# Conversions of the second layer's weights one step behind their raw loads, and the samples' norm with tokens on partitions

## The chip, the cores and the metric

The kernel runs on one core of one Trainium2 chip. The metric is the device time of one execution in microseconds (us). Before the change the median of three runs is 2826.94 us (2825.27 to 2832.05). All engines of the core work at once, each through its own list of instructions in a fixed order: TensorE (PE in the profile; its weight loads are PEld), VectorE (DVE), ScalarE (ACT), GpSimd (POOL) and SyncE (SP), which here only issues transfers.

## The reference

One inference step of a two-layer decoder for two groups of tokens that share the weights: a prompt of 2048 tokens and 8 samples of 4 tokens each (32 rows). The model width is 1024.

- Layer 0 is gated linear attention with 4 heads (keys of 128, values of 512): `o, state = gla_recurrence(q, k, v, log_a, state0)`, then `o = rmsnorm(o, out_norm_g)` per head, then `(o * silu(gate)) @ w_out`. The samples start from given states, the prompt from zero.
- Keys and values for layer 1 are projected once from the residual after layer 0 (`w_k`, `w_v`).
- Layer 1 is sliding-window attention (128 previous positions and the token itself) with 32 query heads of 64 in 4 groups: `q, gate = split(rmsnorm(h) @ b_w_in)`, attention with sinks, `(o * silu(gate)) @ b_w_out`.

The two places that the change touches are the weights of layer 1 (`w_k`, `w_v`, `b_w_in`), which have to be brought into the form that the matmuls read, and the per-head `rmsnorm` of the samples' readout `o` in layer 0: the mean of 512 squares for each of the 32 tokens, to the power -1/2, times `o`.

## The kernel before, in words

All large matmuls work on numbers split into two 16-bit halves, a high and a low one (`split`, L185 to L193): ScalarE writes the high half with one activation (L189 or L192), VectorE writes the rest, the difference, as the low half (L190 or L193). A product is three passes of 16-bit matmuls (`PASSES`).

A `Unit` (L195 on) is a piece of 1024 weight columns in two halves of 512. `Unit.convert` (L207) takes one half: it loads the raw 32-bit numbers into a tile `wraw` of 128x512 (three buffers) with one or two transfers from SyncE's queue, and splits them, scaled by the gain of the norm, into the tile that it is given. For layer 0's weights this tile is a `W` tile that stays on the chip (`load`, L230). Layer 1's weights don't fit beside layer 0's, so `prepare` (L235) converts them in advance: it takes a tile `pst` (two buffers), calls `convert`, and writes `pst` to a tensor `pre` in the chip's memory with a transfer from GpSimd's queue (L243). Much later `fetch` loads the finished pieces in one transfer each. There are 72 such halves: 8 of `w_k` and `w_v` (two transfers each) and 64 of `b_w_in`.

Work in layer 0 runs in 16 blocks: for each head h (4) the four quarters j of the prompt (512 tokens). A block projects v and the gate for four chunks of 128 tokens and q and k of the block after it, takes seven masked `lev` products (`level_steps`), and runs the state recurrence (`chunk_steps`). The last quarter of each head (j = 3) also projects the samples (`SampleA.proj_steps`) and loads the next head's `W` tiles; the samples' own recurrence (`SampleA.steps`: `diag`, `level`, `mid`, `stack`, eight times `seq`, `fin`) is spread over the first quarter of the next head (for the last head over the first chunks of the output projection). It uses `pst` tiles too: `stack`, each `seq` and `fin` take one.

After the last block come 16 chunks of layer 0's output projection (`a_out`), then layer 1.

Where the order of the work comes from: the program is written as lists of steps that `weave` lays into each other, and a planner (`TileContext(nc, schedule_with_timeline_sim=True)`) then makes each engine's list from it, by priorities and by its own durations for every instruction and transfer. Steps in `behind(steps, n)` have their priority lowered by n. What is ready early by the planner's reckoning may be moved ahead of what stands before it in the program; `tc.keep_in_program_order` forbids this for one instruction: it adds an order-only edge from the instruction of the same engine that precedes it in the program text.

The preparation of layer 1's weights is a list `prep` of small steps (L869): 8 steps for the rotary tables, the 72 halves of `prepare`, each lowered by 200, and 64 steps that form combinations of `b_w_out`. `some(n)` takes the next n steps; each chunk of a block takes `PR[j]` of them, that is 1, 4, 2 and 0 for j = 0 to 3 (none in the first two blocks and in the last two), and chunks 1 to 3 of the output projection six each. So by the program text 3, 12 and 6 steps fall into the first three quarters of a head.

`fin` of the samples (L784 to L801) for one head: the readout `ot` (128 value rows on the partitions, 4 pieces, 32 tokens along the free axis) is squared on ScalarE; four 32-bit matmuls with a 128x128 matrix of ones as the moved-against operand (`mm(pq, onef, sq[:, x])`) give the sum of squares of each token in all 128 partitions; VectorE scales it (L796), GpSimd raises 128x32 numbers to the power -1/2 (L797), and VectorE multiplies the gate and the readout (L799) and the result by the power (L800).

## Time and profile before

| | |
|---|---|
| median of the runs | 2826.94 us (2825.27 to 2832.05, three runs) |
| the profiled execution | 2821.32 us, of which 2819.5 us lie between its first and last instruction |
| mean granted TensorE clock | 0.988 |
| 0 to 340 us | head 0 with its loads and norms: PE busy 297.15 us |
| 340 to 1260 us | heads 1 to 3 and the first chunks of the output projection: PE busy 886.63 of 920 us |
| 1260 to 1500 us | rest of the output projection: PE busy 239.76 of 240 us |
| 1500 to 2819.5 us | layer 1 |

How to read it. The span is the time from the first to the last instruction of one profiled execution. A row of the windows view gives, for one stretch of the span, how long each engine was busy in it and the clock that TensorE was granted. A row of a timeline has the start, the duration, the engine, the line, and the tile written and the tiles read; a bracket at its end gives the idle time of that engine just before, and what ended it. "DMA pre<-pst" is a transfer from a `pst` tile, "L218 wraw<-in_b_w_in_dram" the raw load of a half.

### The profile page before, as it was taken

The page shows a single profiled execution, that of the slowest core. Times are in us where ns is not written, and L with a number is a line of the kernel's source. Part 1 is how long each engine was busy: PE and PEld are TensorE (multiplying, and loading weights), DVE is VectorE, ACT ScalarE, POOL GpSimd, SP SyncE. Part 2 cuts the span into 40 slices and gives each one's busy share as a digit, 9 for nine tenths or more (in the row PEclk, how much of TensorE's full clock was granted, in tenths as well). Part 3 has the DMA queues.
Part 4 walks back from the last instruction along what each step waited for, and adds up shares of the span by engine and source line. Part 5 has one row for each costly group of instructions (what it writes and reads, how often), then busy time and mean ns, then how long its engine had stood idle before and what let it go on. Part 6 is the DMA issues. An engine that isn't in the chain of part 4 may idle for free.

```text
span 2819.5 us, 51844 instructions
## 1 busy us (share of the span) xinstructions
PE 2712.2 (96%) x19258; PEld 1388.1 (49%) x19258; DVE 1699.8 (60%) x3470; ACT 1394.2 (49%) x3245; POOL 1150.2 (41%) x1600
## 2 busy tenths in 40 slices
PE   6899999999999999999999999999999999989999
PEld 3444544544454445445444555555555555544444
DVE  5555666566556654346413666677777767777653
ACT  6554656455546554434312555566666666651110
POOL 2442244223323421236304686566557657530000
PEclk9999999999999999999999999999999999999999
DMA  8462445135423543789856787978978889896431
GB/s 213 94 148 50 116 130 163 49 105 154 131 57 105 173 115 93 211 256 287 244 167 161 130 153 151 228 133 152 198 143 149 169 181 183 166 222 197 151 110 57
DMA packets 814470, 429.53 MB, mean 152 GB/s; under 512 B 649600, under 2 KB 723144, under 8 KB 814184
## 3 DMA queue, kind: packets, MB, share of 16 engines
q1 hardware_dynamic: 801256, 390.49, 58.9%
q0 software_dynamic: 10880, 35.66, 3.5%
q8 instruction: 150, 2.46, 0.4%
q14 instruction: 104, 0.85, 0.1%
q10 hardware_dynamic: 2080, 0.07, 0.0%
HBM read 178.75 MB, written 107.54 MB: 102 GB/s over the span
## 4 chain that ended last, share of the span: by engine, by line
PE 62%; ACT 8%; DMA 7%; issue 7%; DVE 6%; POOL 5%; SPq 1%; ACTq 0%; POOLq 0%; DVEq 0%
PE pj L102 36%; PE o L102 11%; PE tr L102 10%; PE kv L102 3%; DMA pre<-pst 2%; ACT o L1264 2%; PE lev L102 2%; DVE v L193 1%; ACT v L192 1%; DMA pst<-v 1%; POOL ogT L190 1%; DMA uT<-ogT 1%; DVE o L1259 1%; DVE lev L1259 1%; POOL rs_r L182 1%
## 5 line engine op out<-in xcount | busy, mean ns | idle before, releaser
L102 PE MATMUL pj<-W,uT 128*128 128x512 f16 x5088 | 1207.2, 382 | 7.8 <-ACT sg L482 6.0
L102 PEld LDWEIGHTS <-uT 128*128 128x128 f16 x6976 | 651.7, 98 | 714.4 <-issue 44.2
L102 PE MATMUL tr<-W,uT 128*128 128x512 f16 x1536 | 365.5, 379 | 0.0
L181 POOL TENSOR_SCALAR rs_m<-ss 128x1 f32<-128x1 f32 (+3 forms) x186 | 42.8, 230 | 548.4 <-DVE ss L1161 190.1
L102 PEld LDWEIGHTS <-X 128*128 128x128 f16 x2744 | 184.7, 98 | 140.4 <-issue 11.4
L1264 ACT ACTIVATE o<-o,mx 128x256 f32<-128x256 f32 (+1 forms) x384 | 168.7, 439 | 168.6 <-DVE mx L1259 164.7
L1259 DVE CUSTOM_DVE_ANT_0 o<-o,madd,nsink 128x256 f32<-128x256 f32 (+1 forms) x384 | 183.7, 478 | 44.6 <-PE o L102 40.4
L102 PE MATMUL pj<-uT,W 128*128 128x512 f16 (+1 forms) x912 | 186.1, 352 | 25.3 <-DMA uT<-ogT 24.4
L193 DVE SCALAR_TENSOR_TENSOR v<-o,v 128x512 f16<-128x512 f32 (+1 forms) x192 | 128.9, 671 | 104.0 <-ACT v L192 101.3
L182 POOL TENSOR_TENSOR rs_r<-rs_m,mhalf 128x1 f32<-128x1 f32 (+3 forms) x182 | 185.5, 1020 | 13.6
L515 POOL TENSOR_TENSOR KQ<-KQ,bt 128x256 f32<-128x256 f32 x112 | 97.5, 870 | 213.1 <-DVE X L190 213.1
L102 PEld LDWEIGHTS <-W 128*128 128x128 f16 x2448 | 127.7, 98 | 111.6 <-issue 19.1
L102 PEld LDWEIGHTS <-v 128*128 128x128 f16 x976 | 96.0, 99 | 120.4 <-issue 9.9
L190 POOL TENSOR_TENSOR ogT<-og,ogT 128x512 f16<-128x512 f32 x68 | 80.8, 1189 | 133.7 <-ACT ogT L189 133.7
L102 PEld LDWEIGHTS <-sg 128*128 128x128 f16 x800 | 77.8, 98 | 92.5
L189 ACT ACTIVATE X<-KQ 128x512 f16<-128x512 f32 x128 | 84.5, 660 | 74.1 <-PE lev L102 53.3
L190 DVE TENSOR_TENSOR X<-KQ,X 128x512 f16<-128x512 f32 x128 | 99.6, 778 | 28.0 <-ACT X L189 25.5
L102 PE MATMUL o<-gl,X 128*128 128x256 f16 (+1 forms) x768 | 114.4, 272 | 1.9 <-DMA gl<-KVd 1.2
L192 ACT ACTIVATE v<-o 128x512 f16<-128x512 f32 (+1 forms) x192 | 111.2, 579 | 3.5
L243 POOL DMA_DIRECT2D pre<-pst x72 | 51.1, 725 | 144.5 <-DVE pst L193 85.8
L1264 ACT ACTIVATE lev<-lev,mx 128x256 f32<-128x256 f32 (+1 forms) x128 | 56.5, 441 | 103.3 <-DVE mx L1259 101.2
L102 PE MATMUL pj<-W,v 128*128 128x512 f16 x448 | 105.6, 383 | 0.0
(437 smaller groups left out, 4848.9 us busy)
## 6 DMA issues: line engine op xcount, KB each, us to landing
pre<-pst POOLq DMA_DIRECT2D x72, 256.0 KB, 3.6
W<-pre SPq DMA_DIRECT2D x36, 512.0 KB
ogd<-ogk SPq DMA_DIRECT2D x68, 256.0 KB
wraw<-in_a_w_in_dram SPq DMA_DIRECT2D x64, 256.0 KB
wraw<-in_b_w_in_dram SPq DMA_DIRECT2D x64, 256.0 KB
oge<-og SPq DMA_DIRECT2D x64, 256.0 KB
wraw<-in_a_w_out_dram SPq DMA_DIRECT2D x32, 256.0 KB
X<-in_x_prompt_dram SPq DMA_DIRECT2D x32, 256.0 KB
```

Of the source, the lines that this page charges most:

```text
L102: return order(nc.tensor.matmul(*a, **k))
L181: pool.tensor_scalar(m[:n, :k], ss, a, b, ALU.mult, ALU.add)
L182: pool.tensor_tensor(r[:n, :k], m[:n, :k], mhalf[:n, :k], ALU.pow)
L189: act(hi, src, AF.Copy)
L190: eng.tensor_tensor(lo, src, hi, ALU.subtract)
L192: act(hi, src, AF.Copy, scale=sc)
L193: dve.scalar_tensor_tensor(lo, src, sc, hi, ALU.mult, ALU.subtract)
L243: nc.gpsimd.dma_start(self.pre[:, :, half * 512 : half * 512 + 512], t)
L515: pool.tensor_tensor(keys, keys, d[:, :, 1:2].to_broadcast([P, NB, m]), ALU.mult)
L1259: dve.tensor_tensor_reduce(pm[:, z], pm[:, z], madd.rearrange("p a b -> p (a b)")[:, (2 - nk) * P :], -0.125, nsink[:, g * GRP + h : g * G ...
L1264: act(pm[:, z], pm[:, z], AF.Exp, scale=-1.0, bias=nm_[:, h : h + 1], accum_out=bx["sum"][:, h : h + 1])
```

## The change

`Unit.convert` is cut into `raw`, which issues the raw loads, and `convert`, which splits. A step of `prepare` now issues its own raw load, then runs what the step before it left in the list `pending`, and leaves its own conversion there: the `pst` tile, the split and the write to `pre`. A `flush` step behind the last half runs what is left, so `prep` has one step more. The ScalarE activation of these conversions, and only of these, is passed through `tc.keep_in_program_order`. The conversions of layer 0's weights (`load`) keep raw load and split in one step, and are not held in program order.

In the samples' `fin` the four matmuls change their operands: the squares are now the loaded matrix and one column of ones the moving one, so that the sums of the 32 tokens stand on 32 partitions, one number each. They are copied to `ss` (VectorE), scaled and raised to the power -1/2 by `rsqrt` (L179 to L183, GpSimd, one number on each of 32 partitions), spread on a 32x32 diagonal `dg` (VectorE), and brought back to all 128 partitions by a fifth matmul `pr`, with ones; the last product reads `pr` in place of the tile `k1`.

```diff
-    def split(dst, src, sc=None, eng=dve):
+    def split(dst, src, sc=None, eng=dve, put=lambda x: x):
...
-            act(hi, src, AF.Copy, scale=sc)
+            put(act(hi, src, AF.Copy, scale=sc))
             dve.scalar_tensor_tensor(lo, src, sc, hi, ALU.mult, ALU.subtract)
+
+    pending = []
+
+    def flush():
+        while pending:
+            pending.pop(0)()
...
-        def convert(self, half, dst):
+        def raw(self, half):
...
+            return raw
+
+        def convert(self, half, raw, dst, put=lambda x: x):
...
         def load(self, half):
...
-            self.convert(half, lambda hl: self.t[:, hl, half * 512 : half * 512 + 512])
+            self.convert(half, self.raw(half), lambda hl: self.t[:, hl, half * 512 : half * 512 + 512])
...
             def one(half):
-                t = T("pst", [P, 2, 512], F16, 2)
-                self.convert(half, lambda hl: t[:, hl])
-                nc.gpsimd.dma_start(self.pre[:, :, half * 512 : half * 512 + 512], t)
+                raw = self.raw(half)
+                flush()
+
+                def rest():
+                    t = T("pst", [P, 2, 512], F16, 2)
+                    self.convert(half, raw, lambda hl: t[:, hl], tc.keep_in_program_order)
+                    nc.gpsimd.dma_start(self.pre[:, :, half * 512 : half * 512 + 512], t)
+
+                pending.append(rest)
...
-                pq = PT("tr", [P, SMP], bufs=2)
+                pq = PT("tr", [SMP, 1], bufs=2)
                 for x in range(4):
-                    mm(pq, onef, sq[:, x], start=x == 0, stop=x == 3)
+                    mm(pq, sq[:, x], onef[:, 0:1], start=x == 0, stop=x == 3)
                 k2 = SOG**-2.0
-                r = T("k1", [P, SMP], F32, 2)
-                dve.tensor_scalar(r, pq, k2 / DV, k2 * EPS * OA * OA * DK, ALU.mult, ALU.add)
-                pool.tensor_tensor(r, r, mhalf[:, 0:1].to_broadcast([P, SMP]), ALU.pow)
+                ss = T("ss", [P, 3], F32, 4)
+                dve.tensor_copy(ss[:SMP, 0:1], pq)
+                r = rsqrt(ss[:SMP, 0:1], SMP, k2 / DV, k2 * EPS * OA * OA * DK)
+                dg = T("k1", [SMP, SMP], F32, 2)
+                dve.tensor_scalar(dg, idf[:SMP, :SMP], r[:SMP, 0:1], None, ALU.mult)
+                pr = PT("tr", [P, SMP], bufs=2)
+                mm(pr, onef[:SMP], dg, start=True, stop=True)
...
-                dve.tensor_tensor(sg, sg, r.unsqueeze(1).to_broadcast([P, 4, SMP]), ALU.mult)
+                dve.tensor_tensor(sg, sg, pr.unsqueeze(1).to_broadcast([P, 4, SMP]), ALU.mult)
...
-    prep = [f for w in gw for f in w.prepare()] + [f for m in range(8) for f in form_steps(m)]
+    prep = [f for w in gw for f in w.prepare()] + behind([flush], 200) + [f for m in range(8) for f in form_steps(m)]
```

## The prediction

> **What bounds the kernel now.** I read the page first, then the windows by stage and by block, then the gaps of TensorE (PE) one by one, and for each what ScalarE (ACT) was doing.

> ```profile
> span 2819.5 us, 51844 instructions
> PE 2712.2 (96%) x19258; PEld 1388.1 (49%) x19258; DVE 1699.8 (60%) x3470; ACT 1394.2 (49%) x3245; POOL 1150.2 (41%) x1600
> ```

> PE is the bound, and the change takes no PE work away that counts, so it can only win PE's idle time and the time in which PE's clock is halved. The windows by block of heads 1 to 3 (cut where PE starts the projections of a block) say where these lie:

> ```profile
> core 0: us, PE busy (x) PEld busy (x) DVE busy (x) ACT busy (x) POOL busy (x), PEclk, DMA share, GB/s
> ...
> 415.00:485.00 70.00, 63.42 (x361) 29.13 (x360) 47.67 (x74) 45.03 (x75) 34.39 (x54) 0.98 0.59 173
> 485.00:553.00 68.00, 68.00 (x406) 32.42 (x405) 30.71 (x49) 27.72 (x47) 16.89 (x27) 1.00 0.18 43
> ...
> 688.00:757.00 69.00, 64.07 (x358) 29.21 (x357) 45.74 (x71) 39.80 (x69) 30.96 (x45) 0.95 0.60 176
> 757.00:825.00 68.00, 68.00 (x421) 32.68 (x420) 30.25 (x49) 28.08 (x48) 16.98 (x27) 1.00 0.20 42
> 825.00:888.00 63.00, 62.83 (x493) 31.87 (x490) 40.90 (x66) 38.77 (x70) 17.18 (x29) 1.00 0.41 113
> ...
> 961.00:1030.00 69.00, 61.86 (x355) 28.50 (x353) 46.43 (x67) 39.87 (x66) 25.57 (x38) 0.98 0.59 171
> ...
> 1155.00:1255.00 100.00, 92.17 (x477) 42.51 (x475) 39.07 (x79) 37.49 (x71) 16.89 (x31) 0.95 0.74 227
> ```

> The second quarter of each head (415, 688, 961) loses 6.58, 4.93 and 7.14 us, 18.65 together; the first output chunks (1155 to 1255) lose 7.83; the third quarters (485, 757) lose nothing. To the idle time comes the halved clock behind it:

> ```profile
> 444.60:448.00 3.40, 3.40 (x9) 1.22 (x8) 2.61 (x4) 0.72 (x1) 2.05 (x3) 0.50 0.93 265
> 714.20:717.60 3.40, 3.04 (x8) 1.12 (x8) 2.59 (x5) 0.70 (x1) 2.68 (x4) 0.51 0.98 223
> ...
> 1175.00:1181.90 6.90, 5.97 (x17) 2.33 (x18) 2.25 (x8) 2.54 (x7) 0.00 (x0) 0.51 0.46 125
> 1219.40:1222.80 3.40, 3.40 (x10) 1.24 (x9) 0.26 (x2) 0.88 (x4) 0.75 (x2) 0.51 0.93 311
> sum 23.90, PE 22.61 PEld 8.34 DVE 12.86 ACT 7.53 POOL 7.32; mean PE 3.77 PEld 1.39 DVE 2.14 ACT 1.25 POOL 1.22
> ```

> At half clock half of the busy time is lost: 22.61/2 = 11.3 us over these stretches, of which the two output-chunk rows hold (5.97+3.40)/2 = 4.7 and the second quarters the other 6.6. So the second quarters cost 18.65+6.6 = 25.3 us, the first output chunks 7.83+4.7 = 12.5. These 37.8 us are the most that the change can win. What PE waited for in the larger gaps:

> ```profile
> 442.47 0.38 PE L102 MATMUL kv<-v,ke 128*128 128x512 f16 x1 [2.02 <-ACT v L192]
> 712.88 0.38 PE L102 MATMUL kv<-v,ke 128*128 128x512 f16 x1 [1.40 <-ACT v L192]
> ...
> 1175.93 0.25 PE L102 MATMUL lev<-ssm 128*96 128x16 f16 x1 [3.82 <-ACT ssm L189]
> 1218.30 0.38 PE L102 MATMUL kv<-ke,skn 96*128 96x512 f16 x1 [3.91 <-DVE bt L778]
> ```

> And what ACT did meanwhile, at two of them:

> ```profile
> 441.21 0.72 ACT L192 ACTIVATE pst<-wraw,gsb 128x512 f16<-128x512 f32 x1 [0.80 <-ACT ogT L189]
> 441.84 0.58 ACT L192 ACTIVATE v<-pj 128x512 f16<-128x512 f32 x1
> ...
> 1209.80 0.69 POOL L243 DMA_DIRECT2D pre<-pst  x1 [5.57 <-DVE pst L193]
> 1210.96 0.34 SPq L218 DMA_DIRECT2D wraw<-in_b_w_in_dram  x1
> 1215.98 0.72 ACT L192 ACTIVATE pst<-wraw,gsb 128x512 f16<-128x512 f32 x1 [3.41 <-DMA pre<-pst]
> ```

> A conversion of a layer-1 half stood at the head of ACT's list, waiting for its input or its `pst` buffer, and the activation that PE needed (`v` at 441.84) stood behind it. At 1215.98 the bracket names the write from `pst`, but that was issued at 1209.80; the raw load issued at 1210.96 is the later of the two, and I take it for the real releaser: 5.0 us from issue to use.

> **The change part by part.** First where conversions run. Rows of the `wraw` tile by stretch:

> ```profile
> 417.00:485.00 68.00, 16.17 (x23) 14.04 (x23) 0.00 (x0) 0.97 0.58 171
> 485.00:553.00 68.00, 0.00 (x0) 0.00 (x0) 0.00 (x0) 1.00 0.18 43
> ...
> 676.00:744.00 68.00, 18.57 (x26) 16.27 (x26) 0.00 (x0) 0.95 0.65 197
> ...
> 948.00:1012.00 64.00, 19.37 (x24) 17.14 (x24) 0.00 (x0) 0.97 0.63 191
> ```

> By the program text a second quarter has 12 preparing steps and a third quarter 6. In the trace the second quarters hold 23, 26 and 24 ACT conversions (73; with them some of layer 0's, which queue for the same three `wraw` buffers) and the third quarter none: the planner runs everything ahead as soon as a buffer is free by its reckoning. *Program order* forbids that: a conversion comes behind the activation that precedes it in the text, so each second quarter keeps its 12, and the 6 others, with what queues for `wraw` behind them, go to the third quarter, where PE has no idle time, ACT is busy 27.72 of 68 us and the transfers 0.18. If the loss goes with the number of conversions, the second quarters keep 36/73 of 25.3 us: a gain of 25.3 x 37/73 = 12.8 us. Bounds: 0 (the twelve that stay do all the harm) and 25.3.

> The third quarters then get 3 x 6 = 18 conversions. At the rate of the second quarters (25.3/73 = 0.35 us each) they would cost 6.2 us, at that of their own stage, 0. I take 1, since two conversions per chunk leave ACT time between them.

> *Raw loads one step ahead.* In the first output chunks the number of conversions stays, but each finds its raw half landed. Of the two large gaps there the one at 1218.30 is of this kind: 3.91 us and half of 3.40 us at halved clock, 5.6 us gained. The one at 1175.93 waits for the samples' own `ssm`, and I leave it. Bounds 0 and 12.5. The raw loads themselves change neither number nor size; each is issued one step earlier on SP, and where it waits for a `wraw` buffer the samples' state loads and the transposes of `ogT` and `X` wait behind it on that queue, as they do now.

> What stays is the ring of two `pst` buffers. The rows of that tile, and ACT's wait for the buffer in the waits view (total, times, longest):

> ```profile
> ACT pst L192 <- DMA pre<-pst: 46.7, 25, 4.0
> ...
> L243 POOL DMA_DIRECT2D pre<-pst x72: 671/690/1407, 403.2 to 1255.4; - x72
> L192 ACT ACTIVATE pst<-wraw,gsb x64: 705/721/724, 430.6 to 1252.5; 128x512 f16<-128x512 f32 x64
> L193 DVE SCALAR_TENSOR_TENSOR pst<-wraw,gsb,pst x64: 731/751/1859, 431.3 to 1253.2; 128x512 f16<-128x512 f32 x64
> DMA to landing us min/median/max: 2.3/3.6/6.8
> ```

> A buffer is held for 0.72 (ACT) + 0.75 (DVE) + 0.69 (issue) + 3.6 (landing, which I count from the end of the issue: an estimate on the long side) = 5.8 us, so two buffers allow one conversion in 2.9 us. Nothing in the change touches that.

> *The added wait.* Order alone adds no transfer and no semaphore, but a wait where the conversion waits for the activation ahead of it. Behind a conversion on ACT stand the splits of `v`, `X` and `sth`, for which PE waits; on DVE its low half stands ahead of theirs. The conversion's own reader is the write to `pre` on POOL, needed by no one before layer 1. A `wraw` buffer, however, is now held from its load until the conversion one step later, and from the last step of a third quarter over the whole last quarter, where no step is taken: one of three buffers is missing there for 16 halves of `W`. PE lost 0.17 us in that stretch (825 to 888) and the last of those 16 conversions is

> ```profile
> 881.34 0.71 ACT L192 ACTIVATE W<-wraw,gsa 128x512 f16<-128x512 f32 x1
> ```

> It ends at 882, 6 us before the next head begins at 888. With that cover I put it at 1 us; without it, see the third case below.

> *The samples' norm.* It removes L797, four times, and adds a power like L182:

> ```profile
> L797 POOL TENSOR_TENSOR k<-k,mhalf x4: 5568/5686/6070, 408.7 to 1259.6; 128x32 f32<-128x32 f32 x4
> L796 DVE TENSOR_SCALAR k<-tr x4: 178/181/191, 407.9 to 1258.7; 128x32 f32<-128x32 f32 x4
> L182 POOL TENSOR_TENSOR rs_r<-rs_m,mhalf x182: 540/937/1657, 9.8 to 2487.8; 128x1 f32<-128x1 f32 x100, 128x8 f32<-128x8 f32 x64, 128x4 f32<-128x4 f32 x16, 32x1 f32<-32x1 f32 x2
> ```

> POOL is freed for 4 x (5.69 - 0.94) = 19 us, but PE has none of its larger gaps in these four places, so I count it at nothing: POOL was idle otherwise, and the result is only needed at the samples' output projection. What is new is that PE itself must come back to the chain: the fifth matmul waits in PE's in-order list for a copy, two POOL steps and a product. If the planner puts it too early, PE waits for the rest of that chain. Bounds: 0, and four times the whole chain, 0.94 for the power and some 0.2 for each of three short steps like L796, 1.5 us, so 6. The planner does leave room for the chain, and only its error counts, so I take a third, 2. The fp32 matmuls with one column instead of 32 are not in the trace; the five together lie within a few tenths of a us of the four.

> Sum: -12.8 + 1 - 5.6 + 1 + 2 = -14.4 us. The profiled execution took 2821.3 us (the span of 2819.5 and 1.8 around it), so 2806.9; the median of the runs lies 5.6 us above it, so I forecast 2812.5 us.

> One term hangs on the clock. In the trace the gaps of 2.02 and 1.40 us before 444.6 and 714.2 are followed by 3.4 us at half clock. [...]

> **The rivals.** *The `pst` ring decides* (no change that can be measured). Four steps of a second quarter stand at the end of each chunk, the last four of its 14 woven steps, some 5 of its 69/4 = 17 us, and the ring passes one in 2.9 us, so conversions wait on ACT as now, only in other places. For it: ACT waited 25 times for "DMA pre<-pst", 46.7 us. Against it: the steps are of low priority and may fall back into the next chunk. Half of the first term and of the second go: -14.4 + 6.4 + 2.8 = -5.2, 2822 us. That the pin changes little, because the planner's order was much the same, comes out here too.

> *The held `wraw` buffer decides* (slower). Two buffers for 16 halves of `W` in the last quarter: one buffer's round is 0.72 + 0.75 + 0.34 + about 3.6 (a raw load taken like the write of the same 256 KB) = 5.4 us, so one conversion in 2.7 us in place of 1.8, 14.4 us later over 16. It decides from the point at which this exceeds the 6 us of cover; then 8.4 us of PE idle at each of three boundaries, and three slices of half clock at 3.40/2, 30 us in all: -14.4 + 30 = +16, 2843 us. Against it: these conversions come in bursts, when PE has freed `W` buffers, and the bursts have gaps that take up delay.

> *Everything goes*: the stalls of the second quarters vanish wholly and 1175.93 too: -37.8 + 4 = -34, 2793 us.

> **How the numbers follow.** Forecast 0.52, ring 0.25, held buffer 0.15, everything 0.08. What a measurement of this kernel can tell from no change is about 0.3%, 8.5 us. The forecast (but for 0.02 of its chance) and the last case are faster by more, 0.58; the ring case lies within, 0.27 with those 0.02; the held buffer is slower, 0.15. The range reaches from 2796, short of the last case, to 2833, past the ring case and the forecast with its costs at their upper ends; the slower case lies outside.

> **What would show it.** Right: conversions in 485 to 553 and 757 to 825, some six each; second quarters with about half of their idle time and of their halved slices; brackets before conversions that name no raw load; no 5.7 us power on POOL. Wrong: new PE gaps behind `pr` in `fin`; gaps at the starts of heads 2 and 3 that wait for `W`; waits for "DMA pre<-pst" of the old total; conversions still running ahead.

## The result, and the profile after

The kernel after takes 2805.36 us (median of six runs, 2800.94 to 2805.9), the kernel before beside it 2829.49 us (six runs, 2825.27 to 2833.13): a ratio of 0.991, with a 95% interval of 0.9897 to 0.9922, so 24.1 us less. The forecast was 2812.5 us. The sign, the range, the place of the gain and program order as the larger part came out. The size of that part did not, nor the reason given for the second part, the raw loads one step ahead.

The profiled execution of after took 2805.45 us, about its median. That of before (2821.32) lay 8 us below the median of its runs, so a comparison of these two profiles shows 15.9 us, not 24. The head of the page of after:

```profile
span 2803.6 us, 51849 instructions
...
PE 2705.6 (97%) x19266; PEld 1386.7 (49%) x19266; DVE 1704.4 (61%) x3474; ACT 1392.0 (50%) x3245; POOL 1135.7 (41%) x1604
```

To see where the time went, I cut both executions at the same instructions: at the second `KQ<-pj` activation (L439 before, L457 after) of every second block, and at the first matmul `kv<-gl`, with which layer 1 begins. Heads 1 and 2 then have one row with the first and second quarter (nearly) and one with the third and fourth. The fifth row has the first two quarters of head 3, the sixth its last two and the output projection, the seventh layer 1 (which before the change begins at 1551.50 us, not at the round 1500 of the table further up). Columns are the stretch, its length, the busy time of each engine with the number of its instructions, the clock, and the transfers. First before:

```profile
core 0: us, PE busy (x) PEld busy (x) DVE busy (x) ACT busy (x) POOL busy (x), PEclk, DMA share, GB/s
356.04:502.73 146.69, 139.98 (x863) 66.81 (x862) 92.35 (x154) 80.72 (x141) 62.89 (x88) 0.99 0.48 139
502.73:626.66 123.93, 122.65 (x872) 60.84 (x871) 73.68 (x127) 67.19 (x123) 35.28 (x55) 1.00 0.32 86
626.66:774.04 147.38, 140.86 (x861) 67.11 (x860) 91.75 (x155) 80.56 (x141) 57.53 (x82) 0.98 0.46 138
774.04:898.87 124.83, 123.02 (x873) 61.01 (x872) 73.57 (x127) 68.92 (x124) 34.37 (x57) 1.00 0.35 87
898.87:1047.09 148.22, 139.40 (x861) 66.70 (x860) 93.37 (x153) 81.41 (x140) 53.03 (x76) 0.99 0.46 135
1047.09:1551.50 504.41, 495.95 (x2810) 234.29 (x2809) 212.47 (x337) 170.62 (x341) 159.72 (x227) 0.99 0.68 200
1551.50:2819.50 1268.00, 1237.11 (x10045) 672.68 (x10043) 854.41 (x2050) 640.98 (x1871) 628.17 (x818) 0.99 0.75 160
```

and after, with the same columns:

```profile
356.81:494.69 137.88, 136.83 (x864) 65.93 (x862) 83.70 (x140) 72.22 (x125) 51.35 (x82) 1.00 0.41 113
494.69:620.38 125.69, 123.39 (x873) 60.97 (x872) 83.66 (x141) 75.01 (x138) 42.16 (x63) 1.00 0.45 120
620.38:757.55 137.17, 136.89 (x863) 65.93 (x862) 84.65 (x143) 73.66 (x127) 47.41 (x76) 1.00 0.40 116
757.55:884.26 126.71, 123.39 (x873) 60.99 (x872) 83.32 (x141) 75.40 (x137) 42.33 (x63) 1.00 0.44 119
884.26:1031.89 147.63, 142.22 (x886) 68.15 (x885) 90.84 (x153) 79.56 (x137) 48.60 (x76) 1.00 0.46 129
1031.89:1527.68 495.79, 487.42 (x2787) 230.18 (x2787) 214.71 (x342) 171.21 (x344) 158.41 (x227) 1.00 0.70 206
1527.68:2803.60 1275.92, 1240.33 (x10045) 674.42 (x10043) 854.59 (x2050) 641.10 (x1871) 627.67 (x818) 0.99 0.75 159
```

Length less PE's busy time is PE's idle time. In the three rows with a second quarter it was 6.71 + 6.52 + 8.82 = 22.1 us and is 1.05 + 0.28 + 5.41 = 6.7: 15.3 won. In the two rows with a fourth quarter it rose from 1.28 + 1.81 to 2.30 + 3.32: 2.5 lost. The sixth row has to be cut once more, where the matmuls `o<-uT,uT` of the output projection's first chunk begin. The output projection from there on, before and then after:

```profile
1151.01:1551.50 400.49, 392.42 (x2109) 183.50 (x2108) 159.82 (x253) 124.36 (x254) 136.41 (x191) 0.99 0.74 220
1134.04:1527.68 393.64, 388.34 (x2110) 181.73 (x2109) 159.10 (x254) 123.49 (x254) 133.72 (x192) 1.00 0.76 224
```

Its idle time fell from 8.07 to 5.30 us: 2.8 won. In the two quarters of head 3 ahead of it, idle time rose from 0.39 us (before, 1047.09 to 1151.01) to 3.07 (after, 1031.89 to 1134.04): 2.7 lost. Through the six rows PE's busy time fell as well, from 1161.86 to 1150.14 us, by 11.7, for about the same matmuls (the counts show some 25 moved from the sixth row to the fifth): the stretches at half clock, 11.3 us by the prediction's count, are gone, and PEclk is 1.00 in all six rows. Idle time (12.9 us) and busy time together are 24.6 us. The start of the rows is 0.8 us later, and layer 1 takes 7.9 us longer in this execution, which leaves the 15.9 us of the spans.

Next come the lines that the prediction named as what would show it. These are busy rows of the tile `wraw` (VectorE, then ScalarE), where before the second quarters had 23, 26 and 24 and the third none:

```profile
417.00:485.00 68.00, 9.71 (x12) 8.40 (x12) 0.00 (x0) 1.00 0.48 131
485.00:553.00 68.00, 10.37 (x16) 9.65 (x17) 0.00 (x0) 1.00 0.42 107
676.00:744.00 68.00, 9.26 (x12) 8.40 (x12) 0.00 (x0) 1.00 0.47 135
...
948.00:1012.00 64.00, 10.92 (x14) 9.84 (x14) 0.00 (x0) 1.00 0.49 139
```

The second quarters of heads 1 and 2 have the 12 that the text gives them, head 3's has these and two of layer 0's. In the third quarter of head 1 six of the 17 on ScalarE are layer 1's, as the text has it, and eleven are layer 0's. At the place where `v` had stood behind a conversion (441.84 before), ScalarE's list in after reads

```profile
437.19 0.60 ACT L192 ACTIVATE v<-pj 128x512 f16<-128x512 f32 x1 [1.44 <-PE pj L102]
439.57 0.71 ACT L189 ACTIVATE X<-KQ 128x512 f16<-128x512 f32 x1 [1.79 <-PE lev L102]
440.19 1.32 ACT L192 ACTIVATE pst<-wraw,gskv 128x512 f16<-128x512 f32 x2
```

`v` and `X` now wait for PE, and not PE for them; the conversions come behind. The ring of buffers is hardly less waited for, by the waits view (total, times, longest):

```profile
ACT pst L192 <- DMA pre<-pst: 40.9, 18, 5.9
ACT W L192 <- DMA wraw<-in_a_w_in_dram: 32.3, 29, 2.1
```

The first was 46.7 us in 25 times before. So ScalarE still waits for the ring 40.9 us, while PE's idle time in the second quarters is 6.7 us in place of 22.1: most of this wait must now stand where nothing urgent is behind it. What the writes still cost is measured below.

### The profile page after: what moved, and what is told of

Its sections match the earlier page's. It is cut to its first block, busy times and chain, and to the rows that moved or that the text cites. A ratio compares the mean times of both kernels' runs of the same rounds, so it can differ in the third digit from the quotient of the medians.

```text
span 2803.6 us, 51849 instructions
## 1 busy us (share of the span) xinstructions
PE 2705.6 (97%) x19266; PEld 1386.7 (49%) x19266; DVE 1704.4 (61%) x3474; ACT 1392.0 (50%) x3245; POOL 1135.7 (41%) x1604
## 4 chain that ended last, share of the span: by engine, by line
PE 62%; DMA 10%; ACT 10%; DVE 7%; issue 5%; POOL 5%; SPq 1%; ACTq 0%; POOLq 0%; DVEq 0%
PE pj L102 37%; PE o L102 11%; PE tr L102 9%; PE kv L102 3%; ACT o L1286 2%; PE lev L102 2%; DVE v L193 2%; DMA pre<-pst 1%; DMA wraw<-in_a_w_in_dram 1%; ACT v L192 1%; DMA pst<-v 1%; POOL ogT L190 1%; DVE o L1281 1%; DMA W<-in_state_gla_dram 1%; DMA uT<-ogT 1%
## 5 line engine op out<-in xcount | busy, mean ns | idle before, releaser
L102 PE MATMUL pj<-W,uT 128*128 128x512 f16 x5088 | 1200.6, 381 | 5.9 <-ACT KQ L457 2.4
L102 PEld LDWEIGHTS <-uT 128*128 128x128 f16 x6976 | 651.4, 98 | 701.8 <-issue 28.5
L102 PE MATMUL tr<-W,uT 128*128 128x512 f16 x1536 | 365.5, 379 | 0.0
L102 PEld LDWEIGHTS <-X 128*128 128x128 f16 x2744 | 185.0, 98 | 140.8 <-issue 8.7
L102 PE MATMUL pj<-uT,W 128*128 128x512 f16 (+1 forms) x912 | 187.5, 355 | 27.9 <-DMA uT<-ogT 24.4
L182 POOL TENSOR_TENSOR rs_r<-rs_m,mhalf 128x1 f32<-128x1 f32 (+2 forms) x186 | 186.8, 1004 | 14.1
L193 DVE SCALAR_TENSOR_TENSOR v<-o,v 128x512 f16<-128x512 f32 (+1 forms) x192 | 128.8, 671 | 102.3 <-ACT v L192 100.1
L102 PEld LDWEIGHTS <-W 128*128 128x128 f16 x2448 | 129.1, 98 | 114.7 <-issue 21.3
L102 PEld LDWEIGHTS <-v 128*128 128x128 f16 x976 | 95.1, 98 | 115.9 <-issue 2.4
L189 ACT ACTIVATE X<-KQ 128x512 f16<-128x512 f32 x128 | 84.7, 662 | 83.5 <-PE lev L102 57.4
L102 PEld LDWEIGHTS <-sg 128*128 128x128 f16 x800 | 77.7, 98 | 93.4 <-issue 1.2
L102 PE MATMUL o<-gl,X 128*128 128x256 f16 (+1 forms) x768 | 114.5, 272 | 6.2 <-DMA X<-qe 5.9
L192 ACT ACTIVATE v<-o 128x512 f16<-128x512 f32 (+1 forms) x192 | 111.2, 579 | 3.5
L396 POOL TENSOR_TENSOR bt<-bt 128x256 f32<-128x256 f32 (+6 forms) x112 | 47.1, 420 | 145.6 <-ACT bt L385 138.6
```

Of the source, the lines that this page charges most:

```text
L102: return order(nc.tensor.matmul(*a, **k))
L182: pool.tensor_tensor(r[:n, :k], m[:n, :k], mhalf[:n, :k], ALU.pow)
L189: act(hi, src, AF.Copy)
L192: put(act(hi, src, AF.Copy, scale=sc))
L193: dve.scalar_tensor_tensor(lo, src, sc, hi, ALU.mult, ALU.subtract)
L396: pool.tensor_tensor(dst, two[:, :, 0], two[:, :, 1], ALU.mult)
```

## The experiments

After the result three theories stood against each other. A: the order on ScalarE, that is program order, decides. B: raw halves that have landed one step ahead decide. C: a good part comes from GpSimd's power of 5.7 us in the samples' norm. All ratios are to the kernel before, measured beside each, with 95% intervals. After's own row aside, there were three series, with medians of before of 2827.38 us (the first four), 2829.70 (`pin_bunched` to `pow_one`) and 2829.57 us (the last four).

| kernel | median us | ratio | interval |
|---|---|---|---|
| after (whole change) | 2805.36 | 0.9910 | 0.9897 to 0.9922 |
| conv_only | 2804.68 | 0.9921 | 0.9907 to 0.9936 |
| norm_only | 2836.86 | 1.0035 | 1.0022 to 1.0048 |
| ahead_no_pin | 2825.42 | 0.9990 | 0.9978 to 1.0002 |
| pin_not_ahead | 2800.81 | 0.9909 | 0.9894 to 0.9925 |
| pin_bunched | 2808.65 | 0.9931 | 0.9918 to 0.9943 |
| pin_spread | 2798.24 | 0.9888 | 0.9874 to 0.9901 |
| late_prio | 2832.67 | 1.0008 | 0.9998 to 1.0017 |
| pow_one | 2832.60 | 1.0013 | 1.0002 to 1.0024 |
| no_write | 2817.43 | 0.9963 | 0.9950 to 0.9975 |
| no_write_pin | 2791.87 | 0.9871 | 0.9857 to 0.9884 |
| no_steps | 2788.24 | 0.9854 | 0.9839 to 0.9869 |
| before_again | 2827.80 | 0.9994 | 0.9982 to 1.0007 |

**The change in its two halves.** The conversions alone (`conv_only`: the kernel after with `fin` as before):

```diff
-                pq = PT("tr", [SMP, 1], bufs=2)
+                pq = PT("tr", [P, SMP], bufs=2)
                 for x in range(4):
-                    mm(pq, sq[:, x], onef[:, 0:1], start=x == 0, stop=x == 3)
+                    mm(pq, onef, sq[:, x], start=x == 0, stop=x == 3)
...
+                pool.tensor_tensor(r, r, mhalf[:, 0:1].to_broadcast([P, SMP]), ALU.pow)
...
```

> The kernel before with the conversions' half of the change alone (raw load one step ahead, program order on ScalarE), the samples' norm as before. Theory A (the place of the conversions decides): nearly all of the gain, a ratio to the kernel before of 0.990 to 0.993. Theory C (GpSimd's 5.7 us power holds up the writes from pst, and its removal is a good part of the gain): 0.994 to 0.997.

It has the whole gain: 0.9921. The norm alone (`norm_only`: the kernel before with the new `fin`, the same lines the other way round):

> The kernel before with the samples' norm alone changed. Theory A: no change that can be measured, 0.999 to 1.002. Theory C: 0.994 to 0.997, with fewer TensorE gaps in the second quarters of the heads, since the writes from pst are issued earlier.

It is slower, 1.0035, some 10 us, which no theory had. The fifth matmul explains little of that. It waits in one of its four places; the timeline of PE has there

```profile
1276.00 0.37 PE L102 MATMUL tr<-k,spp 32*128 32x32 f32 x2 [1.91 <-DVE k L799]
```

and 3.4 us at half clock behind it (the window, with PEclk after POOL),

```profile
1277.10:1280.50 3.40, 3.40 (x10) 1.13 (x8) 0.00 (x0) 0.00 (x0) 0.32 (x1) 0.52 0.99 298
```

so 1.91 + 3.40/2 = 3.6 us. The other gaps lie mostly in the second quarters and in the output projection, as before and some of them larger, for instance in ScalarE's list

```profile
711.03 0.72 ACT L192 ACTIVATE pst<-wraw,gsb 128x512 f16<-128x512 f32 x1 [2.36 <-issue]
...
712.23 0.58 ACT L439 ACTIVATE KQ<-pj 128x512 f32<-128x512 f32 x1
```

where PE waits 3.44 us for that `KQ`. Whatever is changed in the program, the planner deals the conversions anew, and without program order one lands in front of another urgent activation. That the rest of the 10 us is such a new deal is argued, not shown. With program order the norm costs nothing that can be measured: after and `conv_only` have overlapping intervals.

To see the power by itself, `pow_one` keeps the old `fin`, but raises one column of 32 (the other tokens get the first one's factor):

```diff
-                pool.tensor_tensor(r, r, mhalf[:, 0:1].to_broadcast([P, SMP]), ALU.pow)
+                pool.tensor_tensor(r[:, 0:1], r[:, 0:1], mhalf[:, 0:1], ALU.pow)
...
-                dve.tensor_tensor(sg, sg, r.unsqueeze(1).to_broadcast([P, 4, SMP]), ALU.mult)
+                dve.tensor_tensor(sg, sg, r[:, 0:1].unsqueeze(1).to_broadcast([P, 4, SMP]), ALU.mult)
```

> The kernel before, with GpSimd's power in the samples' norm on one column of 128 instead of 32 (the other 31 samples get the first one's factor, so that part of the output is left out): the 5.7 us power becomes one of under 2 us, with no fifth matmul, no copy of the sum and no diagonal. It measures theory C's term by itself. Theory C (the power's 5.7 us stand on the path): 4 heads by about 4 us, 2811 to 2818. Theory A (the power is hidden and the norm's loss of 10 us when changed alone comes from the fifth matmul or from the new order of the program): 2824 to 2830. Rival E (any change of the order of the program around the samples moves this kernel by some 10 us, by chance of the planner): a move of over 5 us either way with the second quarters' gaps in other places.

The power shrinks, in the rows of its line, to

```profile
L797 POOL TENSOR_TENSOR k<-k,mhalf x4: 682/973/1119, 409.5 to 1273.0; 128x1 f32<-128x1 f32 x4
```

and the time does not fall, 1.0013. Nor does it move by the 5 us that rival E asks for: it is 2.9 us, so this run does not support the new deal as the cause above. The 4 x 4.7 us of GpSimd were hidden, as far as this kernel can tell, in which an edit of the norm alone moves the time by some 10 us. With program order the answer doesn't hang on that: after and `conv_only` differ in the norm, and their medians by 0.7 us. Theory C is out.

**Order and raw loads apart.** `ahead_no_pin` is `conv_only` without program order:

```diff
-                    self.convert(half, raw, lambda hl: t[:, hl], tc.keep_in_program_order)
+                    self.convert(half, raw, lambda hl: t[:, hl])
```

> The conversions' half without program order: each raw load still one step ahead of its conversion, but the planner may run the conversions ahead as before; old norm. Theory A: the conversions still bunch in the second quarters (22 or more there, none in the third), ratio 0.997 to 1.001. Theory B (what counts is that a raw half has landed when its conversion comes): most of the gain, 0.990 to 0.994, though the conversions stay where they were.

`pin_not_ahead` is `conv_only` with each raw load in the step of its conversion again:

```diff
                 raw = self.raw(half)
-                flush()
...
-                pending.append(rest)
+                rest()
```

> The conversions' half with program order alone: raw load, conversion and write in one step as before, the conversion's ScalarE activation held in program order; old norm. Theory A: the conversions stand in their own quarters (12 and 6), ratio 0.991 to 0.995. Theory B: the conversions wait for raw halves as before, brackets before them name raw loads, 0.997 to 1.002.

The first brings nothing (0.999, with 1 in the interval), the second everything (0.9909). Theory B is out, theory A stands. ScalarE's conversions of `b_w_in` in 340 to 1260 us, with the idle time before them and what ended it, in `ahead_no_pin`

```profile
L192 ACT ACTIVATE pst<-wraw,gsb 128x512 f16<-128x512 f32 x64 | 45.7, 717 | 61.8 <-DMA pre<-pst 31.5 <-issue 18.9 <-DMA wraw<-in_b_w_in_dram 6.4
```

and in `pin_not_ahead`

```profile
L192 ACT ACTIVATE pst<-wraw,gsb 128x512 f16<-128x512 f32 x64 | 45.1, 714 | 34.6 <-DMA pre<-pst 21.2 <-issue 6.9 <-DMA wraw<-in_b_w_in_dram 1.8
```

Waits for the raw load itself were small in both, 6.4 and 1.8 us; loading ahead had little to win. It even costs something: in the two rows with the third and fourth quarters of heads 1 and 2, PE's idle time is 5.62 us in after, 5.34 in `conv_only` and 5.41 in `ahead_no_pin`, but 3.09 and 3.92 in the two executions of before and 2.95 in `pin_not_ahead`.

**Would a lower rank do as well?** `late_prio` leaves the kernel before as it is and lowers these steps by 1000 instead of 200:

```diff
-            return behind([lambda half=half: one(half) for half in range(2)], 200)
+            return behind([lambda half=half: one(half) for half in range(2)], 1000)
```

> The kernel before, with one change: the steps that convert the second layer's weights are put 1000 behind the text's order in the planner's priority instead of 200, with no program order on ScalarE. It tells whether the gain comes from conversions that stand later on ScalarE or from the pin itself. Theory A (it is the conversions standing ahead that costs, and a planner that only ranks them lower still fills ScalarE's free time with them ahead): about 2822 to 2830, conversions still bunched in the second quarters. Rival D (a lower rank would have done as well): 2800 to 2810, with conversions in the third quarters.

It does not, 1.0008. The rows of `wraw` of this kernel still have everything in the second quarter:

```profile
417.00:485.00 68.00, 16.58 (x23) 14.14 (x23) 0.00 (x0) 0.97 0.59 174
485.00:553.00 68.00, 0.00 (x0) 0.00 (x0) 0.00 (x0) 1.00 0.20 46
```

**How many in a quarter?** Both kernels are `pin_not_ahead` with other numbers of steps per chunk:

```diff
-PR = (1, 4, 2, 0)
+PR = (1, 6, 0, 0)
```

> The kernel with the conversions in program order and the raw loads in the same step (2800.8 us), with one change: the program's text gives the three chunks of a head's quarters 1, 6, 0 and 0 steps a chunk instead of 1, 4, 2 and 0, so all eighteen steps of a head (72 conversions) are written into its second quarter, and program order keeps them there. It tells how many conversions stand in a quarter from their being in order. Theory A1 (the number in the quarter decides: the conversions move back into the second quarter, as they stood in the kernel before, and ScalarE waits there for the ring again): about 2820 to 2828, with idle TensorE and half-clock slices in the second quarters (415 to 485, 688 to 757, 961 to 1030). Theory A2 (the order within the quarter decides: a conversion no longer stands ahead of the head's own ScalarE work): about 2800 to 2808, second quarters as full as in the kernel with the old split.

```diff
-PR = (1, 4, 2, 0)
+PR = (1, 3, 3, 0)
```

> The kernel with the conversions in program order and the raw loads in the same step (2800.8 us), with 1, 3, 3 and 0 steps a chunk instead of 1, 4, 2 and 0: one step a chunk less in the second quarter, one more in the third. Theory A1 (number in the quarter): the second quarter's idle time, 69.3 to 70 busy of 70 in the kernel after, leaves little to gain, the third quarters have 67 busy of 68: 2797 to 2803, at most 3 us either way. Theory A2 (order within the quarter): no change within 0.2%. Both allow no change; a loss of over 5 us would speak for the third quarter being as full of ScalarE work as the second was.

With 18, 12 and 9 steps written into the second quarter the ratio is 0.9931, 0.9909 and 0.9888. Between the ends the intervals do not overlap, between neighbours they do. So fewer is better, but one step of some 6 us is no more than what a new deal of the planner may bring. With eighteen, the ratio still stands for 0.0069 x 2829.7 = 19.5 us less than before, which by the expectation speaks for A2. The trace (of the slowest of its five executions, 2814.37 us) does not put this gain where the eighteen stand. Its rows of heads 1 and 2, first and second quarters, cut as above:

```profile
353.72:493.25 139.53, 138.22 (x868) 67.05 (x867) 90.65 (x147) 75.79 (x132) 71.13 (x96) 1.00 0.53 144
615.78:763.10 147.32, 139.42 (x868) 67.22 (x867) 91.89 (x154) 79.43 (x139) 57.27 (x83) 1.00 0.48 136
```

In head 2, where all eighteen conversions stand in the second quarter, the row is as long as before (147.38 us). PE is idle for 7.9 us in it (before 6.5, after 0.28), and ScalarE waits 11.5 us for the ring (before 13.8, after 6.3). Head 3 is alike: 9.2 us idle, 8.8 before. In head 1, where the list begins with rotary tables and only thirteen conversions are left, it is 1.3 us (before 6.7). So inside a quarter A1 holds in this execution: eighteen conversions in order cost about what the conversions out of order had cost, and fewer cost much less. In head 2 the same row has 2.6 us of idle time with twelve (`pin_not_ahead`) and 0.6 with nine (`pin_spread`). What this kernel wins lies in head 1, in the output projection (396.4 us after 400.5 before, with as many conversions), and in head 0, which ends 2.3 us sooner and has none of the six rotary tables that had stood there. How much of the whole gain is the smaller number and how much the order alone is open. `pin_spread` is the fastest of the kernels that do the whole work, 2798.24 us; beside the kernel after (0.9888 against 0.9910, from different series) the intervals just touch.

**The ring, and the floor.** `no_write` is before with only the first unit's two of the 72 writes to `pre` (all units are fetched from there, so layer 1's result is left out). No ScalarE wait for such a write is left in its trace, but the traffic of the writes is gone too; `no_write_pin` is `pin_not_ahead` with the same omission:

```diff
-            self.pre = dr.tile([P, 2, 1024], F16, tag=f"pre{uniq[0]}", name=f"pre{uniq[0]}")
+            first = not shared
+            if first:
+                shared.append(dr.tile([P, 2, 1024], F16, tag=f"pre{uniq[0]}", name=f"pre{uniq[0]}"))
+            self.pre = shared[0]
...
-                nc.gpsimd.dma_start(self.pre[:, :, half * 512 : half * 512 + 512], t)
+                if first:
+                    nc.gpsimd.dma_start(self.pre[:, :, half * 512 : half * 512 + 512], t)
```

> The kernel before, with one change: of the thirty-two steps that convert the second layer's weights only the first unit's two write their halves to DRAM; the others load and convert as before and write nothing, and all units are fetched from the first one's place (so the second layer's result is left out, its work is not). A conversion that waits for a buffer then no longer waits for a write that GpSimd issues. Theory R (what costs is that a conversion stands ahead of the head's own ScalarE work and waits there for the ring of buffers; program order cures it because fewer conversions meet the ring in one quarter): without the writes the old order costs little, 2800 to 2812 us, the second quarters without half-clock slices. Theory O (what costs is the order itself, whatever the conversion waits for): 2820 to 2832 with the second quarters' idle TensorE time as before. In between, each has its share.

> The same omission of writes in the kernel with program order on ScalarE and the raw load in the same step (2800.8 us). Theory R: no wait is left in either kernel, so it is within 5 us of the old order without writes, 2796 to 2806. Theory O: it stays 20 us or more ahead of that one, 2794 to 2804.

`no_steps` leaves the steps of all but the first unit out:

```diff
             def one(half):
+                if not first:
+                    return
                 t = T("pst", [P, 2, 512], F16, 2)
```

> The kernel before, with all but the first unit's two of these steps left out altogether: no raw load, no conversion, no write (all units are fetched from the first one's place, so the second layer's result is left out). It is the floor: what the steps cost in all, and so how much of it program order brings. If program order has brought nearly all of it: 2790 to 2800, a marker at the end of the first layer of 1520 to 1527 us. If the steps still cost in the kernel after, where ScalarE's own late results also hold up TensorE: 2770 to 2788, marker at 1500 to 1515.

The four kernels make a square. Program order is worth 0.0091 x 2829.6 = 25.7 us with the writes (1 to 0.9909) and 0.0092 x 2829.6 = 26.0 us without them (0.9963 to 0.9871). The writes cost 10.5 us without program order and 10.8 us with it. Each of the four has an interval of 3 to 4 us either way; within that the two are separate effects that add up, and order does not work by sparing the ring alone. Theory R (2800 to 2812 us for `no_write`) falls; theory O had the distance between the two kernels right, 20 us or more, but gave the ring nothing: 2817.4 and 2791.9 us both lie below its ranges. The steps cost 41.3 us in all (0.9854): 25.7 by their order, 10.8 by the writes, 4.8 by what remains. The median of `no_steps`, 2788.2 us, falls between the two ranges of its expectation. In the profiles the remainder isn't in layer 0, which ends at 1516.82 us in `no_steps` and at 1515.14 in `no_write_pin`: with order and without writes, the conversions cost layer 0 nothing that shows.

What a place in the list costs when no buffer is waited for shows in ScalarE's list of `no_write`, in the second quarter of head 2:

```profile
701.66 1.69 ACT L192 ACTIVATE W<-wraw,gsa 128x256 f16<-128x256 f32 x4
703.37 1.28 ACT L373 ACT_TABLE_LOAD   x1
704.66 0.63 ACT L373 ACTIVATE bt<-E 128x512 f32<-128x512 f32 x1
705.20 0.89 ACT L192 ACTIVATE W<-wraw,gsa 128x256 f16<-128x256 f32 x2
706.00 0.61 ACT L192 ACTIVATE sth<-st 128x512 f16<-128x512 f32 x1
706.52 1.32 ACT L192 ACTIVATE pst<-wraw,gsb 128x512 f16<-128x512 f32 x2
707.74 0.57 ACT L605 ACTIVATE og<-o 128x512 f32<-128x512 f32 x1
708.22 0.19 ACT L605 ACTIVATION_READ_ACCUMULATOR og<-o 128x1 f32 x1
708.31 0.58 ACT L445 ACTIVATE KQ<-pj 128x512 f32<-128x512 f32 x1
```

There is no bracket, so no wait, in seven us. ScalarE simply works through eight conversions before `KQ` (3.9 us: 1.69 + 0.89 + 1.32), six of layer 0's weights and two of layer 1's, and PE stands:

```profile
708.94 3.07 PE L102 MATMUL pj<-W,uT 128*128 128x512 f16 x7 [3.76 <-ACT KQ L445]
```

In `no_write_pin` the same `KQ` starts at 693.90, with no conversion of weights in the 5 us before it. This may also be why layer 0's conversions, which are not held in program order, left the second quarters too: they use the same three `wraw` buffers, and queue behind conversions that are now late. No run tests it.

**The kernel before once more.** `before_again` has no edit; a second profiled execution.

> The kernel before, unchanged, for a second profiled execution. The first one (2821.3 us) was the fastest of this kernel's executions; the medians are 2827 to 2830. If executions differ by the clock after gaps, this one has other half-clock slices or more of them and is 2824 to 2833 us; the first layer's marker (1551.5 us in the first) tells whether the difference lies in the first or in the second layer, where the kernel after seemed to lose 7.9 us. No difference of the program, so the same gaps within 0.5 us are expected at most places of the second quarters.

Its span is 2828.6 us. The rows of output projection and layer 1, cut as above:

```profile
1054.87:1560.85 505.98, 495.93 (x2809) 234.22 (x2808) 212.50 (x337) 170.53 (x341) 160.59 (x227) 0.99 0.68 199
1560.85:2828.60 1267.75, 1235.64 (x10045) 672.60 (x10043) 853.18 (x2050) 640.65 (x1871) 627.70 (x818) 0.99 0.75 160
```

Layer 1 takes 1267.75 us, as in the first (1268.00), and layer 0 is 9.4 us longer, 1560.85; 5.1 of these lie in head 0, ahead of the first row. Most of the larger gaps are the same within 0.4 us (2.12 for 2.02, 1.40 for 1.40, 3.81 for 3.91). Against this execution after wins 33.2 us in layer 0, 28.8 of them in the six rows, and loses 8.2 in layer 1: 25.0 together, about what the medians say. In layer 1, PE's idle time rose from 30.89 to 35.59 us and its busy time from 1237.11 to 1240.33 against the first execution. Why is open: the text of layer 1 is the same. It took 1269.2 us in `conv_only`, 1272.0 in `pin_not_ahead`, 1268.4 in `pin_spread`, 1275.0 in `norm_only` and 1275.4 in `no_write_pin`. Both kernels with the new norm are among the long ones, but so is `no_write_pin` with the old one, and each has one profiled execution.

## Why the prediction was right and wrong

- *Second quarters, -12.8 us.* Right in place, sign and cause (program order), too small. Idle time fell by 15.3 us, and the 6.6 us of half clock went wholly: 21.9 in place of 12.8. The step that failed is "if the loss goes with the number of conversions": half of them left, but the loss went by more than two thirds. It falls steeply instead: in head 2's row eighteen conversions in order leave PE idle for 7.9 us, twelve for 2.6 and nine for 0.6 (`pin_bunched`, `pin_not_ahead`, `pin_spread`; after, with twelve, has 0.28). The 6.6 us of half clock did not go in proportion to the number either. And `no_write` shows a cost of the place in the list without any wait.
- *Third quarters, +1 us, and the held `wraw` buffer, +1.* Too small. The rows with third and fourth quarters lost 2.5 us of idle time in heads 1 and 2, and those of head 3 lost 2.7: 5.2 in place of 2. In heads 1 and 2 the loss comes with the loads ahead and not with the conversions: `pin_not_ahead` has the same six of them in the third quarters and no loss (2.95 us idle after 3.09). Whether the held buffer does it is not shown; the waits of `W` for its raw load rose from 18.3 to 32.3 us in the waits view, but also to 31.2 in `pin_not_ahead`, which holds no buffer over the last quarter.
- *Raw loads one step ahead, -5.6 us.* The amount came, its cause was wrong. The output projection is 6.9 us shorter (400.49 to 393.64), 2.8 in idle time and 4.1 in busy time, and the gap at 1218.30 is gone. But `pin_not_ahead`, which loads nothing ahead, takes 392.89 us there, so program order brings this by itself. The loads ahead bring nothing measurable in the whole (`ahead_no_pin`, 0.999), though its one profiled execution has 394.05 us in this stretch too; what does that is open. The reading that failed is "I take it for the real releaser". The bracket had been right: the write issued at 1209.80 landed 6.1 us later, at 1215.9, and the conversion began at 1215.98. Counted off, 64 loads against 64 conversions, its own raw half was issued at 1199.43, 16.5 us ahead; the load of 1210.96 belongs to a later one. At 441.21, too, the write issued at 437.83 had landed just before, 3.3 us after its issue. Both conversions waited for the ring. The group of all such conversions had 6.2 us of waits for raw loads in 340 to 1260 us, against 34.7 for the ring.
- *The fifth matmul, +2 us.* In after it costs nothing: it stands at 413.76, 678.30, 943.88 and 1234.10 us, four times without a wait. Alone, in `norm_only`, it cost one gap. *The 19 us of GpSimd at nothing* were right (`pow_one`).
- *The clock.* Counted with the half clock of the trace the first term is 12.8 us, without it 18.65 x 37/73 = 9.5. The first came nearer to the 21.9 us that went: the 6.6 us of half clock in these stretches went wholly with the gaps. The prediction names the gaps of 2.02 and 1.40 us ahead of 444.6 and 714.2; PE's idle time in the 3.41 us ahead of these two places was 2.03 and 1.71 us (last section).
- *The rivals.* The ring as the decider, with no change that can be measured, is refuted by the result and the square; its statement that ScalarE waits for the ring "as now, only in other places" is true (40.9 us), but it doesn't follow that PE does. In layer 0 the 23.8 us won against the first execution lie about midway between the forecast (14.4) and "Everything goes" (34), the 33.2 against the second at the latter.
- *The total.* For the profiled execution the sum gave 2806.9 us, and it took 2805.45, by two misses that cancel: layer 0 gained 23.8 us and not 14.4, and layer 1 lost 7.9 us, which no step had. In layer 0 the first term gave 9.1 us more, the output projection 1.3 more and the fifth matmul cost 2 less, while third and fourth quarters cost 3.2 more. The 7.1 us between the forecast and the median come with the 5.6 us added for a median above the profile: that held for the execution of before, while the one of after stands at its median. That -5.6 for the raw loads is near the 6.9 us won in the output projection is chance.

## What to carry to other kernels

A conversion that nobody needs yet cost more by its place in the engine's list than by all else (25.7 of the 41.3 us of these steps came with their order): look at which urgent instruction stands behind it, and hold the fill-in work in program order rather than rank it lower, which here changed nothing. Spread it in the program text as well: eighteen conversions in one quarter cost in order about what they had cost out of order, nine or twelve much less. Before a wait is made a term of a sum, take the group's total of that wait, not one gap, and look up when each candidate landed, not only when it was issued; and test a ring by leaving out what it waits for, since most of a long wait that stands in the right place can be free (in `pin_not_ahead` 39.2 us of waits for 10.8 us of cost). Where two profiled executions of one kernel differ by 9 us, compare the medians, and cut both traces at the same instructions to see where the difference lies.

## What the runs showed of the hardware that was not expected

```profile
1001.00:1004.41 3.41, 0.84 (x4) 0.32 (x4) 3.41 (x6) 1.93 (x3) 1.11 (x1) 1.00 0.94 221
1004.41:1007.82 3.41, 3.41 (x10) 1.22 (x9) 2.76 (x5) 1.96 (x3) 0.54 (x1) 0.50 0.71 220
```

After, cut in the same way along its own stretches at half clock (the last of layer 0 ends at 184.77 us), the piece with the gap of 1.77 us had 1.77 us of idle time, and the next one stayed at full speed:

```profile
925.47:928.88 3.41, 1.64 (x10) 0.61 (x8) 1.01 (x2) 1.67 (x4) 0.00 (x0) 1.00 0.64 169
928.88:932.29 3.41, 3.41 (x41) 1.91 (x40) 3.41 (x8) 2.14 (x5) 0.00 (x0) 1.00 0.47 172
```

These are the counts for the full-speed pieces of layer 0 from 340 us on in the two traces. Before, five had over 2.0 us of idle time (2.03 to 2.97), and each was followed by half clock; of seven with 1.5 to 2.0 us one was (1.71 us, at 710.87), of 194 with less none. After, four had 1.69 to 1.77 us and 207 had under 1.5, and none was followed by half clock. Why the piece with 1.71 us was, and one with 1.95 us (at 983.94) was not, is open, and these counts are of two executions.

GpSimd's power in the samples' norm took 5.69 us for 128x32 numbers before, and 0.97 us for 128x1 in `pow_one`.
